# One-layer hybrid trunk on one core: the gated branch's token weights loaded through the ring of raw weights, and half of the Toeplitz copies issued from GpSimd's queue

## The chip, the cores and the metric

The kernel runs on one core of one Trainium2 chip. The metric is the device time of one execution in microseconds, given as the median of several runs. The engines are named as the profile names them: PE is TensorE (matrix multiplies), DVE is VectorE, ACT is ScalarE, POOL is GpSimd, SP is SyncE. PEld is TensorE's weight load, and SPq and ACTq are the instructions on the queues of SP and ACT that issue transfers.

## What is computed

One layer of a sequence model on x of 2048 positions by 1024 channels, in float32. Three branches share one projection; their outputs are normalised, joined and multiplied by W_out, and a mixture of experts follows.

```python
def hybrid_mixer(h, ...):
    z = rms_norm(h, norm_g) @ w_in
    y_a = mixer_spatial_gating(z[..., OFF_A_U:OFF_A_V], z[..., OFF_A_V:OFF_B_X],
                               a_v_norm_g, a_spatial_w, a_spatial_b)
    y_b = mixer_rglru(z[..., OFF_B_X:OFF_B_G], z[..., OFF_B_G:OFF_C_X], ...)
    y_c = mixer_s5(z[..., OFF_C_X:IN_COLS], ...)
    y = jnp.concatenate([rms_norm(y_a, ...), rms_norm(y_b, ...), rms_norm(y_c, ...)], axis=-1)
    return y @ w_out

def mixer_spatial_gating(u_raw, v_raw, v_norm_g, w_s, b_s):
    """per head, within blocks of 128 positions: u * (W_s v + b)"""
    ...
    w = jnp.where(mask[None], w_s, 0.0)      # chunk-causal mask, chunks of 64
    sv = jnp.einsum("hij,bnjhd->bnihd", w, v) + b_s.T[:, :, None]
    return u * sv.reshape(bsz, seq, A_WIDTH)

h = h + hybrid_mixer(h, ...)
h = h + hierarchical_moe(rms_norm(h, norm_ffn_g), ...)   # 16 experts, two of them for each position
```

`w_s` is `a_spatial_w`, six matrices of 128 x 128 (384 KB in all): the token weights of the gated branch A. Branch B is a short convolution and a gated linear recurrence, branch C a complex diagonal state-space layer (S5), which the kernel computes in pieces of 8 positions: inside a piece with a small block Toeplitz matrix, between pieces with a scan.

## The kernel before

**Stages.** x comes in as sixteen tiles of 128 positions and is normalised and transposed (tiles `xT`). Then come the projections by w_in in seven column chunks for each half of 1024 positions, the first half in the order A0, C0, B0, B1, B2, A1, A2. A projection is a group of 24 matmuls in lines 90 to 92 (`split3`: a float32 product as three reduced ones, over eight pieces of the depth); their outputs are called `z`, with shapes 128x512 for B and C and 128x276 for A1. The W_out phase with the router follows, and from about 770 us on the experts.

**What sets the order.** Every engine runs its instructions in the order in which the program wrote them, and waits where an operand isn't ready. The order is written by a main loop over the chunks, which between groups of matmuls gives turns ("ticks") to generators that write the other work piece by piece. A table `TURNS`, keyed by a generator's number and its step, holds back some steps by so many ticks. The generators that matter here:

- `wgen` (generator 1) loads each chunk's raw weights in two halves of 512 KB from SP's queue (`load_w_raw`, L189 to L196) into a pool `raw` with two buffers, and splits them into a high part by ACT (L212) and a low part by DVE (L171, a helper that also serves other lines). For some chunks GpSimd adds 20 router columns (L219 and a subtraction).
- `s5_consts` (L391) computes the constants of branch C and writes them to DRAM tables: `cstP` and `cstT`, and `kpad`, the padded kernel of the Toeplitz matrix. Eight transfers at L738 then spread `kpad` into slot 2 of `cstP`, each 16 x 16 x 128 floats from DRAM to DRAM; those with an odd number go from ACT's queue, the even ones from SP's. After them it loads `a_spatial_w` by two transfers on SP (L742) into two work tiles `big`, gives up eight ticks, transposes the six matrices on PE (L747), copies them to `wsT` on DVE (L748) and zeroes the masked quarter on DVE (L749). It then sets "s5c".
- `c_batch` (L778) works through branch C in eight batches. Each one reads its tables back on SP: `cpp` (L782), `ct` (L783) and, one tick later, `cpm` (L786, slots 2 to 4 of `cstP`, so it needs all eight Toeplitz transfers). On PE stand then the transposes of `zk` (L790, evicted by ACT at L791 to `cx`), the products with `cpp` (L796, "u"), on DVE the scan, on PE the outputs with `cpm` (L815 to L817, "y", evicted by ACT at L818 to `yt`) and a small swap (L825).
- `b_post` (L899) evicts branch B's `z` (ACT L914, `bgg`), multiplies by two gate matrices (PE L920, `bd`), evicts these by ACT (L921, `btr` and `bti`), scans on DVE, and sums squares on PE with a column of ones (L945), for which ACT first squares (L941).
- `c_post` (L831) ends a half of branch C: transposes of `yt` (L851), their eviction (L852, `yc`), the GLU matmuls (L860), sums (L877).

The main loop waits for "s5c" before it begins chunk A1 of the first half.

**DRAM tables and order of transfers.** A transfer that reads a table waits, at its issue, for the landing of those that wrote it. An engine that waits at an issue holds all that stands behind it in its own order, be it transfers or arithmetic.

The code that issues the copies and loads the token weights:

```python
for s in range(8):
    (A if s % 2 else nc.sync).dma_start(out=cstP[s * 16:(s + 1) * 16, 2, :, :], ...)
done.add("s5t")
for h in range(2):
    ws = big[h].rearrange("p (h j) -> p h j", j=P)[:, 0:3, :]
    nc.sync.dma_start(out=ws, in_=io["a_spatial_w"][0, h * 3:h * 3 + 3].rearrange("h i j -> i h j"))
yield 8
```

Of the kernel before, what the change touches and what calls it, by code (L numbers as in the profile page):

```python
# [9 lines left out]
F32 = mybir.dt.float32  # L10
# [3 lines left out]
AF = mybir.ActivationFunctionType  # L14
# [5 lines left out]
P = 128  # L20
# [71 lines left out]
    nc.tensor.matmul(ps, al, bh, start=False, stop=last)  # L92


TURNS = {(32, 2): 0, (40, 12): 0, (1, 119): 5, (29, 3): 5, (21, 4): 3, (13, 4): 1, (17, 14): 3, (28, 6): 2, (26, 7): 3, (17, 2): 0, (33, 1): 2, (12, 9): 3, (25, 7): 1, (28, 9): 2, (28, 11): 3, (21, 9): 0, (44, 4): 0, (35, 97): 3, (32, 3): 0, (48, 9): 1, (38, 4): 0, (41, 2): 2, (14, 6): 1, (18, 15): 2, (37, 1): 3, (1, 132): 0, (48, 5): 0, (35, 85): 2, (9, 1): 0, (44, 8): 0, (49, 7): 2, (27, 8): 2, (29, 1): 2, (25, 3): 0, (47, 11): 5}
RING = 9
NST = 2

# [1 line left out]
class Flow:  # L100
# [12 lines left out]
    def tick(self):  # L113
# [7 lines left out]
        while act:  # L121
            for it in list(act):
                try:
                    r = next(it[0])
                    it[3] += 1
                    r = TURNS.get((it[2], it[3]), r)
                    if r == 0:
# [17 lines left out]
def phases12(tc, io, hd, hc, tab, gcol, ident, c8, stg):  # L145


    nc = tc.nc
    V, A, G, T = nc.vector, nc.scalar, nc.gpsimd, nc.tensor
    ctx = ExitStack()  # L150
    with ctx:
# [7 lines left out]
        rawp = pool("raw", 2)  # L159
        uvp = pool("uvp")  # L160
        psz = pool("psz", 4, space=PSUM)
        pst = pool("pst", 2, space=PSUM)
# [3 lines left out]
        bank = lambda p, nm: p.tile([P, 512], F32, name=nm, tag="b")  # L166
# [22 lines left out]
        def load_w_raw(n):  # L189
            src, cols, _ = chunks[n]  # L190
            m = 256 // len(cols)
            r = []
            for kk in range(2):
                raw = rawp.tile([P, 4, 256], F32, name="raw")
                for j, c in enumerate(cols):
                    nc.sync.dma_start(out=raw[:, :, j * m:(j + 1) * m],  # L196
                                      in_=src[kk * 512:(kk + 1) * 512, c:c + m].rearrange("(k p) n -> p k n", p=P))
                r.append(raw)
            return r

        def wgen():
            for n in range(len(chunks)):
                raws = load_w_raw(n)
                yield
                while begun[0] < n - 1:
                    yield
                w = wp.tile([P, 2, 8, 276], F32R, name="w")
                for k in range(0, 8, 2):
                    rw_ = raws[k // 4][:, k % 4:k % 4 + 2, :]
                    for j in range(2):  # L210
                        g = col(chunks[n][2], k + j)
                        A.activation(w[:, 0, k + j, 0:256], rw_[:, j], AF.Copy, scale=g)  # L212
                    for j in range(2):
                        stt(w[:, 1, k + j, 0:256], rw_[:, j], col(chunks[n][2], k + j), w[:, 0, k + j, 0:256].bitcast(F32), OP.mult, OP.subtract)
                    yield
                if n in routed:
                    while "rw" not in done:
                        yield
                    G.tensor_copy(w[:, 0, :, 256:276], routed[n])  # L219
                    tt(w[:, 1, :, 256:276], routed[n], w[:, 0, :, 256:276].bitcast(F32), OP.subtract, G)  # L220
                wt[n] = w
                if 6 <= n < 14:
                    yield from route_w(n - 6)
            done.add("w")

        def route_w(k):

            raw = rawp.tile([P, 8, P], F32, name="raw")
            nc.sync.dma_start(out=raw, in_=wo[k * P:(k + 1) * P, :].rearrange("p (m n) -> p m n", n=P))
            yield  # L230
            pp_ = []
            for kk in range(2):
                ps = bank(pst if kk else psm, "tp").rearrange("p (k n) -> p k n", n=P)
                for j in range(4):
                    T.transpose(ps[:, j, :], raw[:, kk * 4 + j, :], ident)
                pp_.append(ps)
            for kk in range(2):
                A.activation(raw[:, kk * 4:kk * 4 + 4, :], pp_[kk], AF.Copy)
            yield
            ps = bank(psm, "m")  # L240
            for j in range(8):
                T.matmul(ps[:, 0:20], raw[:, j, :], rw[:, j, :], start=j == 0, stop=j == 7)
            g = col("mix_out_norm_g", k)
            ts(rwy[:, k, :], ps[:, 0:20], g, None, OP.mult)
# [127 lines left out]
        wsT = base.tile([P, 6, P], F32, name="wsT")  # L372
# [14 lines left out]
        cstP = drp.tile([P, 5, 16, P], F32, name="cstP")  # L387
        cstT = drp.tile([P, 2, 16, 129], F32, name="cstT")
        kpad = drp.tile([16, 16, 15, 16], F32, name="kpad")

        def s5_consts(pp):  # L391
# [51 lines left out]
            ps = bank(pst, "tp")  # L443
# [8 lines left out]
            ps = bank(pst, "tp")  # L452
# [154 lines left out]
            for j in range(2):  # L607
                ps = bank(pst, "tp")
# [7 lines left out]
            e = eo[:, 16:19]  # L616
# [76 lines left out]
            big = [big2[:, i * 512:(i + 1) * 512] for i in range(4)]  # L693
# [3 lines left out]
            for g in range(0, 16, 4):  # L697
                dst = lambda slot: cstP[:, slot, g:g + 4, :]

                i = g // 4 % 2  # L700
# [15 lines left out]
                ps = bank(pst, "tp").rearrange("p (a b) -> p a b", b=P)  # L716
# [13 lines left out]
                ps = bank(psm, "tp").rearrange("p (a b) -> p a b", b=P)  # L730
# [4 lines left out]
                nc.sync.dma_start(out=kpad[:, g:g + 4], in_=kp)  # L735
                yield
            for s in range(8):
                (A if s % 2 else nc.sync).dma_start(out=cstP[s * 16:(s + 1) * 16, 2, :, :], in_=kpad[:, :, s:s + 8, :].rearrange("c g t e -> c g (t e)"))  # L738
            done.add("s5t")
            for h in range(2):  # L740
                ws = big[h].rearrange("p (h j) -> p h j", j=P)[:, 0:3, :]
                nc.sync.dma_start(out=ws, in_=io["a_spatial_w"][0, h * 3:h * 3 + 3].rearrange("h i j -> i h j"))  # L742
            yield 8
            for h in range(2):
                ps = bank(pst, "tp").rearrange("p (h j) -> p h j", j=P)
                for j in range(3):
                    T.transpose(ps[:, j, :], big[h][:, j * P:(j + 1) * P], ident)  # L747
                V.tensor_copy(wsT[:, h * 3:h * 3 + 3, :], ps[:, 0:3, :])  # L748
            V.memset(wsT[64:128, :, 0:64], 0.0)  # L749
            done.add("s5c")  # L750
            yield

# [623 lines left out]
        open_pool("prep")  # L1376
        F.add(xprep(2))
        F.add(s5_consts(pools["prep"]))

        def pipeline(lst):  # L1380
# [8 lines left out]
        n = 0  # L1389
# [46 lines left out]
        for h in range(2):  # L1436
            F.until(lambda: ("r", h) in done)
            for m in range(4):
# [4 lines left out]
                for t in range(8):  # L1443
# [16 lines left out]
                    g = h * 8 + t  # L1460
# [499 lines left out]
def trunk(tc, io, out):  # L1960
    nc = tc.nc
    with tc.tile_pool(name="outer", bufs=1) as po, tc.tile_pool(name="c8", bufs=2) as c8, tc.tile_pool(name="odr", bufs=1, space=DRAM) as pd:
        tab = po.tile([P, 368], F32, name="tab")
        gcol = po.tile([P, 8], F32, name="gcol")
        ident = po.tile([P, P], F32, name="ident")
        make_identity(nc, ident)
        hd = pd.tile([S + P, D], F32, name="hd")
        hc = pd.tile([S, D + 16], F32, name="hc")
        stg = []
        phases12(tc, io, hd, hc, tab, gcol, ident, c8, stg)  # L1970
        moe(tc, io, hd, hc, out, tab, gcol, ident, stg)
# [25 lines left out]
```

## Time and profile before

| | |
|---|---|
| time, median of 3 runs | 1603.42 us (1600.23 to 1604.23) |
| the profiled execution | 1600.41 us, of which its span is 1598.6 us |
| PE busy | 1492.4 us, 93% of the span |
| DVE busy | 986.4 us, 62% |
| ACT busy | 864.5 us, 54% |
| POOL busy | 471.1 us, 29% |
| chain that ended last, by engine | PE 74%, DVE 13%, DMA 5%, ACT 4% |

The span is the time from the first to the last recorded instruction; the 1.8 us beside it belong to the same execution. The chain that ended last is followed back from the last instruction to what released each step, so its shares say what the time was spent on, where the busy shares say only how much each engine worked. A row of a timeline gives the start and the length in us, the engine, the line, the operation with output and inputs, and in brackets for how long the engine sat idle before it and which instruction ended that.

### The profile page before, as it was taken

The numbers are of one execution on the slowest core, as the hardware profiler recorded it, in microseconds if no ns is written. First come the engines' busy times: TensorE is split into PE (matmuls) and PEld (weight loads), VectorE is DVE, ScalarE is ACT, GpSimd is POOL, SyncE is SP. The second block draws the span as 40 slices with busy tenths as digits, with TensorE's granted clock in tenths as the row PEclk, the third lists the DMA queues.
The fourth block names the chain that finished last, engine by engine and source line by source line (L and its number), as shares of the span: only waits on it lengthen the run. The fifth ranks groups of instructions, "written<-read, shape, count | busy, mean of one in ns | idle before, by whom it ended". The sixth has DMA issues, their size and how long they took to land.

```text
span 1598.6 us, 25576 instructions
## 1 busy us (share of the span) xinstructions
PE 1492.4 (93%) x8373; PEld 1286.7 (80%) x8374; DVE 986.4 (62%) x2011; ACT 864.5 (54%) x1913; POOL 471.1 (29%) x396
## 2 busy tenths in 40 slices
PE   7998879999999999997799899999999999999993
PEld 6866678878899989997588678888888888888882
DVE  6588661674543487887879886668888857303001
ACT  6377543677544534312346546666566665666662
POOL 0132000000000000010355436555555555445442
PEclk9999888999999999998799899999999999999997
DMA  6247632313532726707577887679888877534342
GB/s 179 66 92 139 188 113 76 123 53 105 166 106 73 264 80 233 281 28 265 200 226 233 248 254 202 201 209 278 269 234 230 250 218 209 139 71 111 89 111 77
DMA packets 213774, 267.46 MB, mean 167 GB/s; under 512 B 34824, under 2 KB 178384, under 8 KB 213648
## 3 DMA queue, kind: packets, MB, share of 16 engines
q1 hardware_dynamic: 187808, 201.95, 39.9%
q0 software_dynamic: 24480, 62.27, 16.1%
q10 hardware_dynamic: 1360, 1.57, 0.3%
q8 instruction: 78, 1.28, 0.3%
q14 instruction: 48, 0.39, 0.1%
HBM read 217.09 MB, written 76.94 MB: 184 GB/s over the span
## 4 chain that ended last, share of the span: by engine, by line
PE 74%; DVE 13%; DMA 5%; ACT 4%; issue 2%; SPq 1%; POOL 0%; POOLq 0%; ACTq 0%; DVEq 0%
PE pg L1688 23%; PE z L90 8%; PE z L92 8%; PE z L91 8%; PE pd L1729 4%; PE pd L1728 4%; PE pd L1727 4%; DMA stg<-in_expert_w_up_dram 2%; DVE ring L1614 2%; DVE ring L1596 2%; PE pt L1695 2%; DVE w L171 1%; PE m L920 1%; PE pt L1700 1%; PE ph L1695 1%
## 5 line engine op out<-in xcount | busy, mean ns | idle before, releaser
L1688 PE MATMUL pg<-ring,xs 128*128 x2016 | 487.3, 394 | 11.8 <-DVE ring L1614 10.6
L1688 PEld LDWEIGHTS pg<-ring,xs 128*128 128x128 f32 x2016 | 378.1, 189 | 91.6 <-issue 14.0
L90 PE MATMUL z<-w,xT 128*128 128x256 f32 (+1 forms) x848 | 250.2, 295 | 4.5 <-DVE ht L171 3.2
L92 PE MATMUL z<-w,xT 128*128 128x256 f32 (+1 forms) x848 | 244.3, 288 | 7.2 <-DVE xT L169 7.2
L91 PE MATMUL z<-w,xT 128*128 128x256 f32 (+1 forms) x848 | 244.3, 288 | 0.0
L1596 DVE TENSOR_SCALAR ring<-stg,gcol 128x512 fp32r<-128x512 f32 x242 | 128.5, 592 | 164.8 <-PE pg L1688 86.2
L1614 DVE SCALAR_TENSOR_TENSOR ring<-stg,gcol,ring 128x512 fp32r<-128x512 f32 x248 | 222.2, 956 | 0.0
L92 PEld LDWEIGHTS z<-w,xT 128*128 128x128 f32 x848 | 163.8, 193 | 8.5 <-DVE xT L169 8.5
L90 PEld LDWEIGHTS z<-w,xT 128*128 128x128 f32 x848 | 164.2, 194 | 7.7 <-issue 4.2
L91 PEld LDWEIGHTS z<-w,xT 128*128 128x128 f32 x848 | 164.4, 194 | 1.4 <-issue 1.4
L1727 PE MATMUL pd<-ring,hh 128*128 x336 | 132.1, 393 | 1.7 <-DVE hh L1633 1.7
L1728 PE MATMUL pd<-ring,hh 128*128 x336 | 131.7, 392 | 0.0
L1729 PE MATMUL pd<-ring,hh 128*128 x336 | 131.7, 392 | 0.0
L1892 POOL DMA_INDIRECT hd<-yb,tab x41 | 76.9, 1874 | 182.5 <-ACT yb L1831 182.5
L171 DVE SCALAR_TENSOR_TENSOR w<-raw,vec,w 128x256 fp32r<-128x256 f32 x176 | 82.0, 511 | 61.9 <-ACT w L212 61.8
L1941 POOL TENSOR_TENSOR yb<-yb,gf 128x1024 f32<-128x1024 f32 x40 | 116.9, 2923 | 2.5 <-ACT hu L1856 2.5
L1906 POOL TENSOR_TENSOR hs<-hs,hu 128x256 f32<-128x256 f32 x84 | 99.8, 1188 | 54.4 <-ACT hu L1810 53.7
L90 PE MATMUL z<-xT,w 128*128 128x512 f32 x256 | 110.5, 432 | 0.2 <-ACT xT L298 0.2
L212 ACT ACTIVATE w<-raw,vec 128x256 fp32r<-128x256 f32 x176 | 77.2, 497 | 59.9 <-PE z L92 36.5
L171 DVE SCALAR_TENSOR_TENSOR ht<-z,rsd,ht 128x256 f32<-128x256 f32 x176 | 85.1, 484 | 29.2 <-PE z L92 21.3
L91 PE MATMUL z<-xT,w 128*128 128x512 f32 x256 | 102.2, 399 | 0.2 <-DVE xT L169 0.2
L92 PE MATMUL z<-xT,w 128*128 128x512 f32 x256 | 102.0, 398 | 0.0
(440 smaller groups left out, 2576.7 us busy)
## 6 DMA issues: line engine op xcount, KB each, us to landing
stg<-in_expert_w_gate_dram SPq DMA_DIRECT2D x62, 512.0 KB, 4.3
stg<-in_expert_w_up_dram SPq DMA_DIRECT2D x62, 512.0 KB, 5.8
stg<-in_expert_w_down_dram SPq DMA_DIRECT2D x60, 512.0 KB, 4.5
raw<-in_w_in_dram SPq DMA_DIRECT2D x48, 256.0 KB
raw<-in_w_out_dram SPq DMA_DIRECT2D x24, 512.0 KB
ht<-in_x_dram SPq DMA_DIRECT2D x16, 512.0 KB
yp<-yTd SPq DMA_DIRECT2D x8, 1024.0 KB
hd<-ht SPq DMA_DIRECT2D x16, 512.0 KB
```

What stands on the lines that cost most here:

```text
L90: nc.tensor.matmul(ps, ah, bh, start=first, stop=False)
L91: nc.tensor.matmul(ps, ah, bl, start=False, stop=False)
L92: nc.tensor.matmul(ps, al, bh, start=False, stop=last)
L171: stt = lambda o, a, s, b, o0, o1: V.scalar_tensor_tensor(out=o, in0=a, scalar=s, in1=b, op0=o0, op1=o1)
L1596: x = v.tensor_scalar(out=ring[:, r, 0, sl], in0=src[:, sl], scalar1=g, scalar2=None, op0=OP.mult)
L1614: x = v.scalar_tensor_tensor(out=ring[:, r, 1, sl], in0=src[:, sl], scalar=g, in1=hi, op0=OP.mult, op1=OP.subtract)
L1688: i = t.matmul(pg[f], xx[j // 2], w[j % 2], start=k == 0 and j == 0, stop=k == 7 and j == 2)
L1727: t.matmul(pd[n], hh[:, 0, kf], w[0], start=kf == 0, stop=False)
L1728: t.matmul(pd[n], hh[:, 0, kf], w[1], start=False, stop=False)
L1729: i = t.matmul(pd[n], hh[:, 1, kf], w[0], start=False, stop=kf == 3)
L1906: g.tensor_tensor(out=o, in0=o, in1=hu[:, f * 256:(f + 1) * 256], op=OP.mult).then_inc(s_hm, 1)
L1941: g.tensor_tensor(out=z, in0=z, in1=gf, op=OP.mult).then_inc(p_z, 1)
```

## The change

The token weights are loaded earlier and elsewhere. `wgen` gets a step `spatial_w` after its chunk 2 (B0): it takes a buffer of the pool `raw`, loads all six matrices with one transfer on SP, and a turn later transposes them on PE and evicts them with two ACT copies to `wsT`; DVE zeroes the quarter there. The two loads, the eight ticks, the six transposes, the two DVE copies and the zeroing leave `s5_consts`. The four Toeplitz copies that ACT issued are issued by GpSimd. Two keys of `TURNS` are renumbered by one, since generator 1 has one step more.

```diff
-TURNS = {..., (1, 119): 5, ..., (1, 132): 0, ...}
+TURNS = {..., (1, 120): 5, ..., (1, 133): 0, ...}
...
                 wt[n] = w
                 if 6 <= n < 14:
                     yield from route_w(n - 6)
+                if n == 2:
+                    yield from spatial_w()
             done.add("w")
+
+        def spatial_w():
+
+            raw = rawp.tile([P, 8, P], F32, name="raw")
+            nc.sync.dma_start(out=raw[:, 0:6, :], in_=io["a_spatial_w"][0].rearrange("h i j -> i h j"))
+            yield
+            for h in range(2):
+                ps = bank(pst, "tp").rearrange("p (h j) -> p h j", j=P)
+                for j in range(3):
+                    T.transpose(ps[:, j, :], raw[:, h * 3 + j, :], ident)
+                A.activation(wsT[:, h * 3:h * 3 + 3, :], ps[:, 0:3, :], AF.Copy)
+            V.memset(wsT[64:128, :, 0:64], 0.0)
...
             for s in range(8):
-                (A if s % 2 else nc.sync).dma_start(out=cstP[s * 16:(s + 1) * 16, 2, :, :], ...)
+                (G if s % 2 else nc.sync).dma_start(out=cstP[s * 16:(s + 1) * 16, 2, :, :], ...)
             done.add("s5t")
-            for h in range(2):
-                ws = big[h].rearrange("p (h j) -> p h j", j=P)[:, 0:3, :]
-                nc.sync.dma_start(out=ws, in_=io["a_spatial_w"][0, h * 3:h * 3 + 3].rearrange("h i j -> i h j"))
-            yield 8
-            for h in range(2):
-                ps = bank(pst, "tp").rearrange("p (h j) -> p h j", j=P)
-                for j in range(3):
-                    T.transpose(ps[:, j, :], big[h][:, j * P:(j + 1) * P], ident)
-                V.tensor_copy(wsT[:, h * 3:h * 3 + 3, :], ps[:, 0:3, :])
-            V.memset(wsT[64:128, :, 0:64], 0.0)
             done.add("s5c")
             yield
```

The changed kernel's lines are numbered 14 higher from the new function to the end of `s5_consts` (L738 becomes L752) and 4 higher behind it. The order on ACT where the last constants of branch C are written, before (`bxc`, `btr` and `bti` are tiles of branch B):

```order
L914 ACTIVATE bgg<-z 128x512
L212 ACTIVATE w<-raw,vec 128x256 x2
L738 DMA cstP<-kpad 16x16x128 x4
L941 ACTIVATE bxc<-bgg 128x512
L921 ACTIVATE btr<-m,b_cols 128x512
L921 ACTIVATE bti<-m,b_cols 128x512
```

Now ACT's four issues are gone from between the weights' split and the squaring, and the same four stand on GpSimd behind the zeroing of `kp`, ahead of the router columns of chunk A1's weights (`w<-rw`) and the state updates of branch C (`gst`):

```order
L169 TENSOR_TENSOR m_1501<-m_1501,m_1500 128x576
L743 MEMSET kp 16x4x112
L752 DMA cstP<-kpad 16x16x128 x4
L219 CAST w<-rw 128x8x20
L169 TENSOR_TENSOR w<-rw,w 128x8x20
L169 TENSOR_TENSOR gst<-gst,gtmp 128x2 x8
```

The order on PE at the beginning of chunk A1, before:

```order
L796 MATMUL m<-cx,cpp 128x128 x4
L790 MATMUL tp<-ident,zk 128x128 x2
L747 MATMUL tp<-ident,big_337 128x128 x6
L815 MATMUL m<-cpm,cx 128x128
...
L825 MATMUL tp<-cg,swp 128x2
L796 MATMUL m<-cx,cpp 128x128 x4
L790 MATMUL tp<-ident,zk 128x128 x2
L920 MATMUL m<-bxc,bd 128x512 x2
L90 MATMUL z<-w,xT 128x276
```

and after it:

```order
L800 MATMUL m<-cx,cpp 128x128 x4
L794 MATMUL tp<-ident,zk 128x128 x2
L90 MATMUL z<-w,xT 128x276
...
L819 MATMUL m<-cpm,cx 128x128
...
L829 MATMUL tp<-cg,swp 128x2
L800 MATMUL m<-cx,cpp 128x128 x4
L794 MATMUL tp<-ident,zk 128x128 x2
L924 MATMUL m<-bxc,bd 128x512 x2
L90 MATMUL z<-w,xT 128x276
```

The transposes of the token weights have left, and A1's first group of 24 matmuls stands in their place; behind `bd` stands its second group. At A1's end the order before has a group between the transposes of `yt` and the GLU matmuls:

```order
L851 MATMUL tp<-ident,yt 128x128 x8
L90 MATMUL z<-w,xT 128x276
...
L92 MATMUL z<-w,xT 128x276
L860 MATMUL m<-yc,glu 128x512 x8
```

and after it has none there:

```order
L92 MATMUL z<-w,xT 128x276
L855 MATMUL tp<-ident,yt 128x128 x8
L864 MATMUL m<-yc,glu 128x512 x8
L881 MATMUL m<-ones,yc 128x1 x16
```

A1's last group has moved ahead of the transposes of `yt`. The six transposes now stand on PE inside chunk B0, twelve matmuls behind those of L610:

```order
L92 MATMUL z<-xT,w 128x512
L236 MATMUL tp<-ident,raw 128x128 x6
L90 MATMUL z<-xT,w 128x512
```

On SP the load of `a_spatial_w` stands between the raw weights of chunk 2 and those of chunk 3, and the two loads at L742 are gone from between the Toeplitz copies and the first tables of branch C.

## Rows read from the trace of the kernel before

**Rows 1.** The page's view of the span in 40 equal slices (40 us each): PE's busy share and its granted clock, in tenths.

```profile
PE   7998879999999999997799899999999999999993
PEclk9999888999999999998799899999999999999997
```

**Rows 2.** The view of windows. Columns: the window in us, its length, busy time (and instructions) of PE, PEld, DVE, ACT and POOL, PE's granted clock as a share of full speed, the busy share of the transfer engines, GB/s.

```profile
60.00:80.00 20.00, 20.00 (x90) 16.21 (x89) 12.14 (x62) 4.18 (x9) 6.51 (x17) 1.00 0.18 54
155.00:160.00 5.00, 3.80 (x15) 2.45 (x13) 0.00 (x0) 0.00 (x0) 0.00 (x0) 1.00 0.90 172
160.00:165.00 5.00, 0.63 (x3) 0.64 (x4) 0.00 (x0) 1.89 (x4) 0.00 (x0) 0.68 1.09 175
165.00:170.00 5.00, 5.00 (x15) 4.21 (x16) 1.64 (x4) 4.94 (x7) 0.00 (x0) 0.50 0.79 212
170.00:175.00 5.00, 5.00 (x20) 3.96 (x19) 3.74 (x10) 2.81 (x7) 0.00 (x0) 0.80 1.04 323
...
280.00:720.00 440.00, 432.19 (x3078) 396.82 (x3078) 280.30 (x724) 218.67 (x502) 8.63 (x25) 0.99 0.41 137
```

**Rows 3.** The timeline of ACT from 150 us on, around its Toeplitz issues (ACTq).

```profile
153.02 0.90 ACT L212 ACTIVATE w<-raw,vec 128x256 fp32r<-128x256 f32 x2
157.90 5.16 ACTq L738 DMA_DIRECT2D cstP<-kpad  x4
163.11 0.63 ACT L941 ACTIVATE bxc<-bgg 128x512 f32<-128x512 f32 x1 [9.19 <-DMA cstT<-ang]
...
164.21 0.68 ACT L921 ACTIVATE bti<-m,b_cols 128x512 f32<-128x512 f32 x1
```

**Rows 4.** The timeline of PE in the same stretch: the gate matmuls, the sums of squares, and the u products of the first two batches of branch C.

```profile
154.15 1.88 PE L920 MATMUL m<-bxc,bd 128*128 128x512 f32 x4
...
164.37 1.87 PE L945 MATMUL m<-ones,bxc 128*128 128x1 f32 x8 [5.57 <-ACT btr L921]
...
177.41 1.05 PE L796 MATMUL m<-cx,cpp 128*128 128x128 f32 x8
...
183.63 1.05 PE L796 MATMUL m<-cx,cpp 128*128 128x128 f32 x8
```

**Rows 5.** The timeline of DVE there: the weights' low part, and the first batch's state products (`cv`).

```profile
165.32 0.88 DVE L171 SCALAR_TENSOR_TENSOR w<-raw,vec,w 128x256 fp32r<-128x256 f32 x2 [10.89 <-ACT w L212]
...
179.03 0.75 DVE L169 TENSOR_TENSOR cv<-m,ct 128x256 f32<-128x256 f32 x2
```

**Rows 6.** The timeline of SP's queue there: its four Toeplitz issues, and the issues of the first batch's tables.

```profile
157.90 7.00 SPq L738 DMA_DIRECT2D cstP<-kpad  x4
...
166.25 0.37 SPq L782 DMA_DIRECT2D cpp<-cstP  x1
...
167.99 0.44 SPq L786 DMA_DIRECT2D cpm<-cstP  x1
```

**Rows 7.** The view of one tile: the gathers of the experts' inputs, transfers that GpSimd issues (duration of the instruction in ns, min/median/max, of 45), and the time from their issue to the landing.

```profile
L1888 POOL DMA_INDIRECT xg<-hc,tab x45: 980/1002/1868, 773.0 to 1556.1; - x45
...
DMA to landing us min/median/max: 4.2/5.9/8.1
```

**Rows 8.** The view of one line: ACT's four Toeplitz issues (ns, min/median/max).

```profile
L738 ACTq DMA_DIRECT2D cstP<-kpad x4: 517/610/862, 157.9 to 162.5; - x4
```

**Rows 9.** The timeline of POOL: the router columns of chunk A1's weights.

```profile
149.97 0.67 POOL L219 CAST w<-rw 128x160 fp32r<-128x160 f32 x1 [6.60 <-PE z L92]
```

**Rows 10.** The timeline of PE where the token weights are transposed, up to A1's first group.

```profile
196.85 0.38 PE L790 MATMUL tp<-ident,zk 128*128 128x128 f32 x2
...
199.59 0.55 PE L747 MATMUL tp<-ident,big 128*128 128x128 f32 x3 [1.34 <-DVE gtmp L169]
...
204.34 0.38 PE L825 MATMUL tp<-cg,swp 128*128 128x2 f32 x2 [2.86 <-DVE wsT L748]
...
207.19 0.69 PE L90 MATMUL z<-w,xT 128*128 128x276 f32 x1
```

**Rows 11.** The timeline of DVE there.

```profile
203.73 1.02 DVE L748 COPY wsT<-tp 128x384 f32<-128x384 f32 x2
...
205.28 0.16 DVE L169 TENSOR_TENSOR gtmp<-tp,cs 128x2 f32<-128x2 f32 x1
```

**Rows 12.** The timelines of ACT and PE behind it: the eviction that begins the next chain, and the PE work that waits for that chain's end.

```profile
213.58 0.38 ACT L791 ACTIVATE cx<-tp 128x256 f32<-128x256 f32 x1 [1.01 <-PE tp L790]
...
230.08 1.87 PE L945 MATMUL m<-ones,bxc 128*128 128x1 f32 x8 [5.35 <-ACT yt L818]
```

**Rows 13.** The timelines of ACT and PE at A1's end: the eviction of `yc`, the first matmul of A1's last group, and the GLU.

```profile
254.53 1.09 ACT L852 ACTIVATE yc<-tp 128x512 f32<-128x512 f32 x2 [2.14 <-PE tp L851]
...
254.69 0.38 PE L90 MATMUL z<-w,xT 128*128 128x276 f32 x1
...
257.83 7.03 PE L860 MATMUL m<-yc,glu 128*128 128x512 f32 x16
```

**Rows 14.** The timelines of PE, SP and ACT near the place to which the transposes move: four transposes between projection matmuls, the issue of raw weights (eight transfers), and chunk 3's split.

```profile
71.42 0.60 PE L610 MATMUL tp<-ident,big 128*128 128x128 f32 x4
71.77 0.48 PE L90 MATMUL z<-xT,w 128*128 128x512 f32 x1
...
41.71 32.51 SPq L196 DMA_DIRECT2D raw<-in_w_in_dram  x8
...
84.44 1.70 ACT L212 ACTIVATE w<-raw,vec 128x256 fp32r<-128x256 f32 x4
```

More of the change, by code (lines that the diff above doesn't have):

```diff
@@ L92, in split3 @@
     nc.tensor.matmul(ps, al, bh, start=False, stop=last)
-TURNS = {(32, 2): 0, (40, 12): 0, (1, 119): 5, (29, 3): 5, (21, 4): 3, (13, 4): 1, (17, 14): 3, (28, 6): 2, (26, 7): 3, (17, 2): 0, (33, 1): 2, (12, 9): 3, (25, 7): 1, (28, 9): 2, (28, 11): 3, (21, 9): 0, (44, 4): 0, (35, 97): 3, (32, 3): 0, (48, 9): 1, (38, 4): 0, (41, 2): 2, (14, 6): 1, (18, 15): 2, (37, 1): 3, (1, 132): 0, (48, 5): 0, (35, 85): 2, (9, 1): 0, (44, 8): 0, (49, 7): 2, (27, 8): 2, (29, 1): 2, (25, 3): 0, (47, 11): 5}
+TURNS = {(32, 2): 0, (40, 12): 0, (1, 120): 5, (29, 3): 5, (21, 4): 3, (13, 4): 1, (17, 14): 3, (28, 6): 2, (26, 7): 3, (17, 2): 0, (33, 1): 2, (12, 9): 3, (25, 7): 1, (28, 9): 2, (28, 11): 3, (21, 9): 0, (44, 4): 0, (35, 97): 3, (32, 3): 0, (48, 9): 1, (38, 4): 0, (41, 2): 2, (14, 6): 1, (18, 15): 2, (37, 1): 3, (1, 133): 0, (48, 5): 0, (35, 85): 2, (9, 1): 0, (44, 8): 0, (49, 7): 2, (27, 8): 2, (29, 1): 2, (25, 3): 0, (47, 11): 5}
 RING = 9
@@ L737, in s5_consts @@
             for s in range(8):
-                (A if s % 2 else nc.sync).dma_start(out=cstP[s * 16:(s + 1) * 16, 2, :, :], in_=kpad[:, :, s:s + 8, :].rearrange("c g t e -> c g (t e)"))
+                (G if s % 2 else nc.sync).dma_start(out=cstP[s * 16:(s + 1) * 16, 2, :, :], in_=kpad[:, :, s:s + 8, :].rearrange("c g t e -> c g (t e)"))
             done.add("s5t")
-            for h in range(2):
-                ws = big[h].rearrange("p (h j) -> p h j", j=P)[:, 0:3, :]
-                nc.sync.dma_start(out=ws, in_=io["a_spatial_w"][0, h * 3:h * 3 + 3].rearrange("h i j -> i h j"))
-            yield 8
-            for h in range(2):
-                ps = bank(pst, "tp").rearrange("p (h j) -> p h j", j=P)
-                for j in range(3):
-                    T.transpose(ps[:, j, :], big[h][:, j * P:(j + 1) * P], ident)
-                V.tensor_copy(wsT[:, h * 3:h * 3 + 3, :], ps[:, 0:3, :])
-            V.memset(wsT[64:128, :, 0:64], 0.0)
             done.add("s5c")
```

## The prediction

> **What bounds the kernel now.** I first read the page's slices [rows 1]: PE is busy nearly everywhere at full clock, so a saving on another engine counts only where PE waits for it. PE's share falls and its clock sags in the fourth and fifth slices (120 to 200 us, which hold the constants of branch C) and in the sixth (200 to 240). I then read those stretches as windows and engine by engine. From 280 to 720 us PE is busy 432.19 of 440 us at a clock of 0.99 [rows 2]: what is gained before 280 us is carried to the end, because behind it PE works through a fixed amount without waiting.
>
> The first hole lies at 158 to 164 us. ACT ends its last weight split at 153.92 (153.02 + 0.90), then has nothing to compute until 163.11: the four Toeplitz issues, which begin at 157.90 and take 5.16 us, stand in its order [rows 3]. They are ahead of the eviction `btr`, and PE stands 5.57 us waiting for just that [rows 4]; DVE stands 10.89 us for ACT's next split [rows 5]. Afterwards PE's granted clock is 0.68, 0.50 and 0.80 in three windows of 5 us, where it had been full before [rows 2]: PE fell to the lower of its two levels, 1.2 GHz, after having idled. The second hole lies around 200 us: PE waits 1.34 us ahead of the second half of the token weights' transposes and 2.86 us for DVE's work behind them [rows 10].
>
> **The Toeplitz issues leave ACT.** The squaring at 163.11 can start when the split ends, and `btr` and `bti` when their gate matmuls are done: these start at 154.15 and last 1.88, so end at 156.03 [rows 4]. `bti` then starts at about 156.1 in place of 164.21: 8.1 us earlier [rows 3]. DVE's chain (`w`, recurrence, `cv` at 179.03 [rows 5]) hangs on ACT's and moves as much, `cv` to 170.9. PE alone could gain more: the 5.57 us, and in the windows at 0.50 and 0.80 half of 5 and a fifth of 5 us, together 9.1. But it meets DVE's and ACT's chain again in the batches, so I take the smaller, **8.1 us**.
>
> What is late next there? The tables of branch C. The first batch's `cpp` is issued at 166.25, behind SP's own Toeplitz issues, which start at 157.90 and take 7.00 [rows 6]. Their transfers don't start earlier than now, since all wait for `kpad`. With two fewer loads behind them, `cpp` is issued some 1 us or more sooner, and the first u, now at 177.41 [rows 4], has to wait for it only from 169.3 on. That leaves about 4 us from an issue at 165 for the landing; the gathers take 4.2 at the least from issue to landing [rows 7], so nothing to a microsecond is lost here.
>
> **The same issues on GpSimd.** No row shows such a transfer from GpSimd; the nearest are the gathers, 1.00 us each by the median and 1.87 at most, landing 4.2 to 8.1 us after issue [rows 7]. Four from 157.90 end between 161.9 and 165.4, and the last lands between 165 and 173. Behind them on GpSimd stands the router columns' cast, now at 149.97 [rows 9], which moves to about 162 to 166 and is read first by A1's matmuls, now at 207.19 and after the change near 197: 30 us of cover. The wait that counts is SP's: `cpm` of the first batch waits for all eight landings, and behind it on SP stand the second batch's `cpp` and `ct` and the next raw weights. `cpm` is now issued at 167.99 [rows 6]; the second u, which needs the `cpp` behind it, is at 183.63 [rows 4] and moves to 175.5. With 2.5 to 3 us from the last landing to a landed `cpp`, by the row's ends it is between 7 us early and 1 us late. I put this at **0**, with a transfer of 1.0 us as the median row has it; for a transfer of D us and the longest landing the wait is 4D − 6.5. Each holds 256 pieces of 512 bytes against a gather of 128 rows, which is why D may be above the rows: a rival below.
>
> **The transposes leave the place at 197 us.** In the order A1's first 24 matmuls take their place. They cost 257.83 − 254.69 = 3.14 us [rows 13], and run while PE waits 1.34 and 2.86 us now [rows 10]. DVE is rid of the two copies and the zeroing, 205.28 − 203.73 = 1.55 us [rows 11], ahead of the state's `gtmp` for which PE's next batch waits. Walked through from 196.85: A1's first group to 200.1, the outputs, the swap (which waits for the scan of the batch), the next u and `zk` to 203, the second gate matmul to 205.4 (it waits for DVE's `cv`), A1's second group to 208.5, the outputs and the next u to 211.2. The eviction `cx`, now at 213.58, comes at 211.4. From there an unchanged chain on ACT and DVE leads to the sums at 230.08, where PE waits 5.35 us for its end [rows 12]. So that wait stays, and all behind it is **2.2 us** earlier, with one group of A1 more already done. Bounds: 0, if the chain's other branch (the weights' split, which doesn't move with `cx`) ends last; 4.2, if all of both waits went.
>
> **A1's end.** Since one group is ahead, the GLU no longer stands behind the last group (at 257.83) but directly behind the transposes of `yt`, and waits for their eviction, which ends at 254.53 + 1.09 = 255.62 [rows 13]: **2.2 us** more, between 0 and 3.1 (the group itself).
>
> **The load through the ring.** The buffer that the spatial load takes is set free about 65 us and its transfer is done before 75; SP issues the raw loads around it from 41.71 to 74.2 [rows 14], and DRAM traffic is low there (share 0.18 [rows 2]). Chunk 3's second half has to wait for the buffer until the transposes have read it, about 76, and is read at 84.44 [rows 14]: covered by some 8 us less the transfer. The six transposes stand in a stretch where PE has no gap (20.00 of 20.00 us [rows 2]). Four like them take 0.35 us from their start to the next matmul's, which itself takes 0.48 instead of 0.39 us [rows 14]: 0.43 for four, so **0.65 us lost** for six, carried to the end. The two ACT copies lie beside an ACT busy 4.18 of 20 us there [rows 2], the zeroing on DVE beside 12.14 of 20; both are far ahead of their reader. That's nothing, or 1.5 us at most if the chain of chunk 3's weights ended last. The `TURNS` keys only keep their places.
>
> **The sum.** 8.1 + 2.2 + 2.2 − 0.65 = 11.9 us. From the profiled execution's own 1600.41 that gives 1588.5. This execution lies 3.0 below the median of 1603.42; the prediction is for a median, so 1603.4 − 11.9 = **1591.5**.
>
> **Rivals.** (1) *GpSimd's copies are late by a little.* If each takes 1.7 to 2.8 us (about the gather's longest, to 1.5 times it), the second u waits 4D − 6.5, 0.3 to 4.7 us, and PE falls to the lower clock again, some 2.5 us as in the window at 0.50 [rows 2]. Gain 9 to 4.8, time 1594.4 to 1598.6, say **1597**. For it: twice the pieces of a gather. Against: a gather also has to read its row numbers, and the median is 1.00. The Trainium skill, "SBUF — State Buffer", section "A bandwidth-pool intuition that's wrong (but worth ruling out)", adds that a transfer from GpSimd is starved while VectorE copies (0.62 us alone, 3.1 overlapped); no row here shows that pair, and by 3.1 the sum would be 11.9 − 5.9 − 2.5 = 3.5 us, an estimate by that page.
>
> (2) *Only issuing time is saved.* If the wait in the hole is that of the tables' round trip, the batches can't start sooner, whichever queue issues: ACT is rid of 4 × 0.61 = 2.4 us [rows 8], less the 0.65 of the transposes, and the later groups only fill the waits that remain: gain 1.8, time **1601.6**. For it: the releaser named at ACT's 9.19 us is a transfer of the tables, and the transfer engines are at 1.09 and 0.79 [rows 2]. Against: ACT's and DVE's work that stands behind the issues is branch B's and the weights', which reads no table. The Trainium skill, "DMA: Bandwidth & Descriptors", section "Issuing engines are not separate DMA queues", says just this: starting transfers from several engines saves only the issuer's time, usually small. ACT's row of 9.19 us idle speaks against it here, since an issuer that computes also loses what it waits for.
>
> (3) *Slower: GpSimd's copies hold SP.* One mechanism: the copies, written one after the other on GpSimd, take D each; SP stands at `cpm` until the last has landed, with all tables and raw weights behind it, and PE stands at the second u for 4D − 6.5 plus 2.5 of clock. The gain is gone from D = 4.0 on (16 − 6.5 + 2.5 = 12.0), and the time is over 0.3% longer from D = 5.2. At D = 6 it is 17.5 + 2.5 − 11.9 = 8.1 slower, **1611.5**. For it: nobody has shown what such a copy costs there. Against: it needs over 2.7 times the longest gather [rows 7].
>
> **How the numbers follow.** The forecast, gain 9 to 15 us (1588.4 to 1594.4): 0.60. Rival 1: 0.20. Rival 2, and copies of 2.8 to 5.2 us with it, which end within 4.8 us of now: 0.11. Rival 3: 0.06. More than 15, if PE keeps its full 9.1 and both waits at 200 go: 0.03. A measurement of this kernel can tell about 0.3%, 4.8 us, from no change. So faster 0.60 + 0.20 + 0.03 = 0.83, same 0.11, slower 0.06. The range reaches from 1586, for the bigger gain, to 1598, which takes in most of rival 1, and leaves some 0.19 out.
>
> **What would show it.** Right: no ACTq issue at 154 to 163; `bti` at about 156; no PE wait of 5.57 there and a clock near 1.00 in 160 to 175; four POOL issues of 1 to 2 us each from about 158; `cpm` issued before 172; `wsT` evicted by ACT near 75; PE's sums still waiting 5 us at about 218; a wait of 1 us ahead of the GLU. Wrong: PE waiting for `cpp` at the first or second u (rival 1 or 3 by the length of GpSimd's issues; rival 2 if those are short and tables land late), or PE waiting for chunk 3's weights near 85 to 95 us, which would say that the ring's buffer was held too long.

## The result, and the profile after

The changed kernel takes 1590.12 us (median of 7 runs, 1587.26 to 1594.48) where the kernel before took 1602.13 (7 runs, 1600.23 to 1605.28) on the same chip: a ratio of 0.9926 with a 95% interval of 0.9908 to 0.9944, 12.0 us faster. The profiled execution takes 1590.12 us, its span 1588.3: 10.3 less than the profiled execution before.

The page's slices, PE and its granted clock, beside [rows 1]:

```profile
PE   7998989999999999996899899999999999999993
PEclk9999988999999999998899999999999999999996
```

The windows (columns as in [rows 2]):

```profile
70.00:80.00 10.00, 8.84 (x44) 6.98 (x44) 7.38 (x34) 2.18 (x5) 4.00 (x7) 1.00 0.32 93
...
155.00:160.00 5.00, 5.00 (x20) 3.42 (x19) 2.15 (x5) 4.04 (x7) 0.00 (x0) 1.00 0.91 228
160.00:165.00 5.00, 5.00 (x27) 4.22 (x26) 1.64 (x4) 4.95 (x7) 2.87 (x6) 1.00 0.89 144
165.00:170.00 5.00, 5.00 (x24) 4.09 (x23) 3.48 (x9) 4.01 (x9) 0.53 (x1) 1.00 0.96 221
170.00:175.00 5.00, 3.58 (x19) 2.45 (x18) 4.90 (x10) 2.09 (x5) 0.00 (x0) 1.00 0.95 269
```

The hole at 158 to 164 us is gone, and with it the low clock behind it: 1.00 in all three windows from 160 on, against 0.68, 0.50 and 0.80. But the first line is new: PE, which had no gap from 60 to 80 us [rows 2], is busy for 8.84 of 10 us. ACT's timeline, to be read against [rows 3], and PE's, against [rows 4]:

```profile
156.39 0.90 ACT L212 ACTIVATE w<-raw,vec 128x256 fp32r<-128x256 f32 x2
157.19 0.62 ACT L945 ACTIVATE bxc<-bgg 128x512 f32<-128x512 f32 x1
...
159.44 0.69 ACT L925 ACTIVATE bti<-m,b_cols 128x512 f32<-128x512 f32 x1 [0.17 <-PE m L924]
```

```profile
157.53 1.88 PE L924 MATMUL m<-bxc,bd 128*128 128x512 f32 x4
162.02 0.95 PE L949 MATMUL m<-ones,bxc 128*128 128x1 f32 x8
...
171.44 1.05 PE L800 MATMUL m<-cx,cpp 128*128 128x128 f32 x8
...
175.18 1.10 PE L924 MATMUL m<-bxc,bd 128*128 128x512 f32 x2 [1.61 <-DVE cv L169]
178.88 1.05 PE L800 MATMUL m<-cx,cpp 128*128 128x128 f32 x8
```

The gate matmuls begin 3.38 us later than before, at 157.53, but the second u products 4.75 us earlier, at 178.88. Between them lie 21.35 us where there were 29.48: the removal of ACT's issues is worth 8.13. The late beginning comes from three places: 0.50 is there before any edit acts (the transposes at 71.42 stand at 71.92), 2.06 arise at the six moved transposes, and 0.8 at a lower clock around 145 us. The rows of the second one, from PE and DVE:

```profile
71.92 0.60 PE L624 MATMUL tp<-ident,big 128*128 128x128 f32 x4
...
76.45 0.88 PE L236 MATMUL tp<-ident,raw 128*128 128x128 f32 x6 [1.16 <-DVE big L170]
```

```profile
75.57 0.43 DVE L169 TENSOR_TENSOR big<-big 128x256 f32<-128x256 f32 x1 [1.79 <-POOL big L169]
75.91 0.48 DVE L170 TENSOR_SCALAR big<-tp,sgn 128x256 f32<-128x256 f32 x1
76.31 0.41 DVE L170 TENSOR_SCALAR big<-tp 128x256 f32<-128x256 f32 x1
```

The transposes at 71.92 wrote two banks `tp` (the buffers that take PE's transposes); DVE is to read both, but stands in its own order behind a step that waits 1.79 us for GpSimd. The six transposes want the same two banks, so PE stands 1.16 us until DVE has emptied them. The windows of the third, each from the gate matmuls near 140 us to the next sums, first before, then after (granted clock 0.69 and 0.59):

```profile
137.97:143.29 5.32, 5.32 (x15) 3.60 (x16) 5.28 (x8) 4.38 (x6) 3.75 (x3) 0.69 0.99 139
```

```profile
140.55:146.66 6.11, 6.11 (x14) 4.17 (x15) 6.07 (x12) 5.17 (x7) 3.81 (x3) 0.59 1.01 124
```

GpSimd's issues (timeline, and the view of the line with the time to landing), and SP's, against [rows 6]:

```profile
162.04 2.54 POOL L752 DMA_DIRECT2D cstP<-kpad  x4 [16.11 <-DMA kpad<-kp]
164.58 0.33 POOL L219 CAST w<-rw 128x160 fp32r<-128x160 f32 x1
```

```profile
L752 POOL DMA_DIRECT2D cstP<-kpad x4: 562/586/832, 162.0 to 164.0; - x4
...
DMA to landing us min/median/max: 5.7/5.9/6.3
```

```profile
161.75 2.54 SPq L752 DMA_DIRECT2D cstP<-kpad  x4
168.03 0.36 SPq L786 DMA_DIRECT2D cpp<-cstP  x1
...
170.05 0.37 SPq L790 DMA_DIRECT2D cpm<-cstP  x1
```

An issue costs GpSimd 0.59 us, and the 16.11 us for which it stands there hold nobody: the cast behind it is read some 27 us later. Further on, PE's sums and the GLU, against [rows 12] and [rows 13]:

```profile
223.23 1.87 PE L949 MATMUL m<-ones,bxc 128*128 128x1 f32 x8 [5.29 <-ACT yt L822]
...
247.44 1.03 PE L855 MATMUL tp<-ident,yt 128*128 128x128 f32 x8
248.31 7.03 PE L864 MATMUL m<-yc,glu 128*128 128x512 f32 x16
```

The sums are 6.85 us earlier than before, 2.10 more than at the second u; the GLU 9.52, another 2.67. At the span's end it is 10.3.

### The profile page after: what moved, and what is told of

The parts are those of the page before. It is cut to its first block, busy times and chain, and to the rows that moved or that the text cites. A ratio compares the mean times of both kernels' runs of the same rounds, so it can differ in the third digit from the quotient of the medians.

```text
span 1588.3 us, 25588 instructions
## 1 busy us (share of the span) xinstructions
PE 1489.4 (94%) x8373; PEld 1283.5 (81%) x8374; DVE 976.4 (61%) x2009; ACT 865.6 (54%) x1915; POOL 484.6 (31%) x400
## 4 chain that ended last, share of the span: by engine, by line
PE 74%; DVE 13%; DMA 4%; ACT 4%; issue 2%; POOL 1%; SPq 0%; DVEq 0%; POOLq 0%; ACTq 0%
PE pg L1692 24%; PE z L90 8%; PE z L92 8%; PE z L91 8%; PE pd L1733 4%; PE pd L1732 4%; PE pd L1731 4%; DMA stg<-in_expert_w_up_dram 3%; DVE ring L1600 2%; PE pt L1699 2%; DVE ring L1618 2%; DVE ht L171 1%; DVE w L171 1%; PE m L924 1%; DVE xT L169 1%
## 5 line engine op out<-in xcount | busy, mean ns | idle before, releaser
L1618 DVE SCALAR_TENSOR_TENSOR ring<-stg,gcol,ring 128x512 fp32r<-128x512 f32 x248 | 213.9, 923 | 0.0
L1910 POOL TENSOR_TENSOR hs<-hs,hu 128x256 f32<-128x256 f32 x84 | 106.5, 1268 | 50.1 <-ACT hu L1814 47.8
```

The lines of the kernel that those rows point to most:

```text
L1618: x = v.scalar_tensor_tensor(out=ring[:, r, 1, sl], in0=src[:, sl], scalar=g, in1=hi, op0=OP.mult, op1=OP.subtract)
L1910: g.tensor_tensor(out=o, in0=o, in1=hu[:, f * 256:(f + 1) * 256], op=OP.mult).then_inc(s_hm, 1)
```

## Experiments

Each was timed beside the kernel before, which took 1600.90 us beside the four from "changed again" to "other banks", 1599.46 beside the next three and 1601.22 beside the last two; so the times are compared by their ratios. As the time of a run scatters by several us, three distances on PE, between starts, carry the reading: from the transposes at 71 us to the next (L624 to L732; L610 to L718 in the numbering before), from the gate matmuls at 157 to the second u, and from there to the GLU, with the sums on the way. In us:

| kernel | time, median | ratio to before (95%) | 71 us to next transposes | gate matmuls to second u | second u to sums | second u to GLU |
|---|---|---|---|---|---|---|
| before | | | 23.45 | 29.48 | 46.45 | 74.20 |
| changed | 1590.12 | 0.9926 (0.9908 to 0.9944) | 25.51 | 21.35 | 44.35 | 69.43 |
| changed again | 1590.29 | 0.9933 (0.9913 to 0.9953) | 25.48 | 21.35 | 44.36 | 69.43 |
| queue only | 1592.95 | 0.9949 (0.9931 to 0.9967) | 23.45 | 21.85 | 49.43 | 76.35 |
| ring only | 1597.61 | 0.9972 (0.9953 to 0.9992) | 25.48 | 28.57 | 44.36 | 69.06 |
| other banks | 1585.48 | 0.9908 (0.9888 to 0.9927) | 24.10 | 21.34 | 44.36 | 68.10 |
| sixteen issues | 1590.24 | 0.9950 (0.9935 to 0.9965) | 25.48 | 21.62 | 44.36 | 69.16 |
| all on SP | 1591.20 | 0.9950 (0.9933 to 0.9968) | 25.48 | 21.35 | 44.36 | 69.55 |
| group back | 1589.09 | 0.9946 (0.9928 to 0.9963) | 25.51 | 21.37 | 42.14 | 69.59 |
| copies on ACT | 1598.32 | 0.9982 (0.9967 to 0.9997) | 23.45 | 28.07 | 44.04 | 71.97 |
| banks and group | 1587.49 | 0.9917 (0.9896 to 0.9938) | 24.11 | 21.35 | 42.12 | 69.22 |

**The changed kernel again.** No edit.

> The changed kernel once more, as a yardstick for the three beside it: 1590 us (1587 to 1594), 12 below the kernel before. If the late start of 0.5 us at 72 us and the lower clock at 140 to 150 us of its first profile are chance, this profile has them otherwise; if they belong to the change, it has the same.

It gave 1590.29. Its transposes at 71 us start at 71.52, so 0.4 of the late start was chance; over all runs they start between 70.75 and 72.19. The low clock at 145 us came again: 6.06 us from the gate matmuls at 140 to the sums, against 6.11 in the first profile and 5.32 in the kernel before.

**The queue alone**, in the kernel before:

```diff
-                (A if s % 2 else nc.sync).dma_start(out=cstP[s * 16:(s + 1) * 16, 2, :, :], ...)
+                (G if s % 2 else nc.sync).dma_start(out=cstP[s * 16:(s + 1) * 16, 2, :, :], ...)
```

> The kernel before with the four Toeplitz issues on GpSimd, nothing else. Theory (ACT was held by the wait for kpad and by the four issues, and PE and DVE by ACT): 8.1 us gained, 1594, the first u products about 8 to 9 us earlier, A1's first group still behind the transposes at 197 with the waits of 1.3 and 2.9 us. Rival (only issuing time is saved): 4 x 0.6 = 2.4 us, 1599.7. Rival (the batches' tables end last): the first u stays near 177, under 3 us gained.

The time fell by 8.0 us, to 1592.95, and the distance to the second u by 7.63. That excludes the rival of 2.4 us: the interval's weak end is 5.3 us. That 8.0 and 7.63 agree so well is partly chance, since 2.15 us of the gain are lost again before the GLU (76.35 against 74.20), and the profiled execution, 1595.29 us, is 5.1 faster than the one before. Two things came out on the way. The first u now waits for transfers, because nothing shifted it later (timeline of PE):

```profile
170.59 1.13 PE L796 MATMUL m<-cx,cpp 128*128 128x128 f32 x8 [1.95 <-DMA yTd<-bgg]
```

The releaser named is a store; of what stands around it on SP, the u reads `cpp`, so I take it for that table's landing. And PE's second hole, now at 190 to 200 us, takes the clock down to the lower level, where it had stayed at 1.00 before (windows of this run, then of the kernel before at its hole):

```profile
190.00:195.00 5.00, 3.19 (x19) 2.70 (x18) 4.83 (x14) 1.66 (x4) 0.20 (x1) 0.83 0.58 184
195.00:200.00 5.00, 2.95 (x14) 2.89 (x14) 3.48 (x11) 0.38 (x1) 0.20 (x1) 0.50 0.45 133
200.00:205.00 5.00, 5.00 (x18) 2.93 (x17) 2.88 (x9) 2.56 (x5) 0.00 (x0) 0.65 0.33 102
```

```profile
195.00:200.00 5.00, 2.83 (x23) 2.27 (x22) 4.86 (x13) 2.04 (x5) 0.20 (x1) 1.00 0.38 115
200.00:205.00 5.00, 2.14 (x20) 1.95 (x19) 4.79 (x13) 0.38 (x1) 0.00 (x0) 1.00 0.42 123
```

The lower clock makes its distance to the sums 3 us longer than before.

**The ring alone**: the changed kernel, its four issues on ACT again.

```diff
-                (G if s % 2 else nc.sync).dma_start(out=cstP[s * 16:(s + 1) * 16, 2, :, :], ...)
+                (A if s % 2 else nc.sync).dma_start(out=cstP[s * 16:(s + 1) * 16, 2, :, :], ...)
```

> The changed kernel with the four Toeplitz issues back on ACT: the move of the token weights alone. Theory (A1 one group earlier is worth 2.2 + 2.7 us, the transposes at 76 us cost 2.1 us, and up to 0.8 more by the clock): a net gain of 2 to 3 us, 1599 to 1600, with the wait of about 9 us on ACT back. Rival (the loss at 76 us is hidden in the wait for the tables): 4.9 us gained, 1597. Rival (the two parts need each other): no gain, 1602.

The time is 1597.61, 3.3 below its kernel before, between the first two expectations and unable to choose. The profile does: ACT's hole is back (28.57), the transposes at 76 us cost the same 2.03, and behind the second u the full 5.1 us are gained. The row of ACT, to be read against [rows 3]:

```profile
163.62 0.63 ACT L945 ACTIVATE bxc<-bgg 128x512 f32<-128x512 f32 x1 [8.29 <-DMA cstT<-ang]
```

The parts don't need each other: 8.0 and 3.3 make 11.3, and the whole change gave 10.6 beside them.

**Other banks**: the six transposes write to the second pool of PSUM.

```diff
-                ps = bank(pst, "tp").rearrange("p (h j) -> p h j", j=P)
+                ps = bank(psm, "tp").rearrange("p (h j) -> p h j", j=P)
```

> The changed kernel with the two PSUM banks of the token weights' transposes taken from the other pool, whose order on every engine is the same. Theory (the transposes wait 1.16 us because VectorE hasn't drained the two banks of the first pool, being held by GpSimd's big): that wait is gone, the 0.9 us of work stays, 1.2 us gained on the changed kernel, 1589, and by chance the lower clock at 140 to 150 us too. Rival (the wait is for the load of the weights or for something else that lies before them): the wait stays at 1.2 us, the time at 1590.

The wait is gone (timeline of PE), and the distance from 71 us falls from 25.48 to 24.10:

```profile
74.50 0.82 PE L236 MATMUL tp<-ident,raw 128*128 128x128 f32 x6
```

What is left over the 23.45 of before is 0.65 us for six transposes. So the wait was for the banks and cost 1.4 us. The time is 1585.48, 4.8 below "changed again", and the intervals of the two overlap. Of the difference only these 1.4 are explained. The profiled executions lie further apart, 1582.62 against 1589.76: there 1.3 lie in a shorter stretch from the sums to the GLU where the clock was higher, 2.1 between the GLUs of the two halves, and 3.1 behind the second one. From its start (468 to 483 us) to that of the experts' last products the profiles here last between 1089.2 us (this one) and 1095.8 (the queue alone), 1092.3 in "changed again" and 1095.4 in "banks and group", which has the same banks. So this part isn't shown to be the banks'.

**Sixteen issues**: each of GpSimd's copies cut into four.

```diff
-                (G if s % 2 else nc.sync).dma_start(out=cstP[s * 16:(s + 1) * 16, 2, :, :], in_=kpad[:, :, s:s + 8, :]...)
+                for gs in ([slice(g, g + 4) for g in (0, 4, 8, 12)] if s % 2 else [slice(0, 16)]): (G if s % 2 else nc.sync).dma_start(out=cstP[s * 16:(s + 1) * 16, 2, gs, :], in_=kpad[:, gs, s:s + 8, :]...)
```

> The changed kernel with each of GpSimd's four Toeplitz copies cut into four, sixteen issues for the same bytes. Theory (SP stands at cpm until the last of GpSimd's copies has landed; four issues of 0.6 us leave it 5 us of slack at the second u): at 0.6 us for each the last issue comes 7 us later, cpm is issued at about 177 in place of 170, the second u waits 2 to 3 us for its table, and with the clock behind it the time is 3 to 5 us longer than the changed kernel's, 1593 to 1595, 6 to 9 below the kernel before. Rival (an issue costs by its pieces, so sixteen small ones cost no more than four): cpm stays near 170, no change from 1590. Rival (the clock is lost at every wait there): 1597 or more.

The view of the line, and SP's timeline:

```profile
L752 POOL DMA_DIRECT2D cstP<-kpad x16: 513/516/787, 145.2 to 170.1; - x16
```

```profile
172.05 0.36 SPq L790 DMA_DIRECT2D cpm<-cstP  x1
```

My theory missed. An issue of a quarter costs nearly as much as a whole one (0.52 against 0.59 us), so the rival's reason is wrong too; but three of the first copy's quarters need only earlier parts of `kpad` and went out at 145 us, so the dose was smaller than meant. GpSimd also stood 2.85 us ahead of its last five issues, until one of its own earlier transfers had landed. The last issue, at 170, moved `cpm` by 2.9 us only, counted from the gate matmuls (15.45 us behind them against 12.52). The second u hardly noticed (21.62): there the tables had nearly 3 us to spare. How long four such copies would have to be before SP holds PE isn't settled by this run; at 0.59 us each, with those 3 us in hand, it isn't reached.

**All on SP**: no Toeplitz copy on ACT or GpSimd.

```diff
-                (G if s % 2 else nc.sync).dma_start(out=cstP[s * 16:(s + 1) * 16, 2, :, :], ...)
+                (nc.sync).dma_start(out=cstP[s * 16:(s + 1) * 16, 2, :, :], ...)
```

> The changed kernel with all eight Toeplitz copies on SP, none on GpSimd or ACT. Theory (what counts is that ACT doesn't stand at the issues; which queue issues them then costs only what it delays behind them): ACT's wait is gone as in the changed kernel, the first table is issued 2 to 3 us later than 168, the first u waits for it, 1 to 2.5 us longer than the changed kernel, 1591 to 1593. Rival (GpSimd's own queue makes the transfers themselves sooner): 5 us or more longer, 1595 or later, with the tables landing that much later.

SP takes 7.80 us for the eight, the first table goes out 11.83 us behind the gate matmuls instead of 10.50, and the first u waits for it (timelines of SP and PE):

```profile
161.89 7.80 SPq L752 DMA_DIRECT2D cstP<-kpad  x8
169.80 0.54 SPq L786 DMA_DIRECT2D cpp<-cstP  x1
```

```profile
172.76 1.13 PE L800 MATMUL m<-cx,cpp 128*128 128x128 f32 x8 [0.70 <-DMA cpp<-cstP]
```

At the second u nothing is left of it (21.35), for PE then waits less for DVE's `cv` (0.66 us against 1.61). By its ratio, 0.9950, the time is no different from the changed kernel's. GpSimd's queue shows no merit of its own; what counts is that ACT doesn't stand at the issues.

**The group back**: A1's first group behind the second gate matmul again.

```diff
-            done.add("s5c")
+            yield 8; done.add("s5c")
```

> The changed kernel with eight ticks of generator 'constants' put back before it lets chunk A1 begin, so that A1's first group stands behind the second gate matmul as before and its last one between the transposes of yt and the GLU, with the token weights' transposes still early. Theory (most of the 4.8 us behind 192 us is the group itself: 2.1 at the sums, 2.7 at the GLU): the GLU is 3 to 4 us later than in the changed kernel, 251.5, and the time 1593 to 1594. Rival (the gain is VectorE's 1.55 us of copies and the transposes' 0.9 us that left this place, and the group only fills what would be idle): under 1.5 us later, 1590 to 1591.5.

The theory fell. The time is 1589.09, and PE's rows show why:

```profile
220.26 1.86 PE L949 MATMUL m<-ones,bxc 128*128 128x1 f32 x8 [5.35 <-ACT yt L822]
...
247.71 7.03 PE L864 MATMUL m<-yc,glu 128*128 128x512 f32 x16
```

Counted from the second u, the sums come 4.3 us earlier than before (42.14 against 46.45) rather than 2.1, and the GLU is where it was in the changed kernel (69.59 against 69.43). Where the group stands moves 2.2 us from one side of the sums to the other and is worth nothing in all. The gain lies in the transposes and their evictions leaving.

**Copies on ACT**, in the kernel before: the transposes stay at 197 us, their copies leave DVE.

```diff
-                V.tensor_copy(wsT[:, h * 3:h * 3 + 3, :], ps[:, 0:3, :])
-            V.memset(wsT[64:128, :, 0:64], 0.0)
+                A.activation(wsT[:, h * 3:h * 3 + 3, :], ps[:, 0:3, :], AF.Copy)
+            G.memset(wsT[64:128, :, 0:64], 0.0)
```

> The kernel before with the token weights' two copies on ScalarE and the zeroing on GpSimd, the transposes left at 197 us. It splits the 4.8 us gained behind 192 us, since A1's group turned out to be worth nothing. Theory (VectorE's 1.55 us of copies and zeroing stood ahead of the state update that PE's next batch waits for): the wait of 2.86 us falls to about 1.3, the sums at 230.1 come 1.5 us earlier, the rest of the 4.8 belongs to the transposes' own 0.9 us and their waits for banks. Rival (the transposes hold PE until the bank is free, whoever copies): under 0.5 us at the sums. By the time 1598 to 1600, too little to tell from no change.

More than expected: the sums come 2.4 us earlier (44.04 against 46.45). PE's wait of 2.86 us ahead of the swap is wholly gone:

```profile
198.44 0.55 PE L747 MATMUL tp<-ident,big 128*128 128x128 f32 x3 [1.11 <-ACT wsT L748]
...
200.16 0.28 PE L825 MATMUL tp<-cg,swp 128*128 128x2 f32 x2
```

So it wasn't DVE's 1.55 us of work that PE waited for but a bank: the swap writes to the bank that the first copy empties, and DVE reached it only at 203.73 [rows 11], behind a whole batch's scan; the swap starts at 204.34, while the second copy still runs. The remaining 1.9 of the 4.3 go when the transposes leave too. The hole of ACT, ahead of this edit, is shorter in this run as well:

```profile
162.19 0.63 ACT L941 ACTIVATE bxc<-bgg 128x512 f32<-128x512 f32 x1 [7.79 <-DMA cstT<-ang]
```

**Banks and group**: both edits on the changed kernel.

```diff
-                ps = bank(pst, "tp").rearrange("p (h j) -> p h j", j=P)
+                ps = bank(psm, "tp").rearrange("p (h j) -> p h j", j=P)
...
-            done.add("s5c")
+            yield 8; done.add("s5c")
```

> The changed kernel with the transposes' banks from the other pool, as in the run on other banks, and A1's first group back behind the gate matmuls. Theory (the banks' wait is worth 1.2 us and the group nothing): no wait at 75 us, GLU at about 246.5, time 1586 to 1589. Rival (the other-banks run's 4.8 us below the changed kernel is all its own): 1585. Rival (it was chance, and the wait was covered): 1590.

24.11, 21.35 and 69.22 us, the GLU at 245.37 (245.25 with other banks alone), 1587.49 us: the banks' 1.4 again, and again nothing from the group. The two kernels with other banks have the lowest ratios; by their times alone neither is told from the changed kernel.

## Why the prediction was right, and where it wasn't

**ACT's issues, 8.1 us: right.** 8.13 in the profile after. The three kernels that keep the issues on ACT show 28.07 to 29.48 to the second u and those that don't 21.34 to 21.85, so the term is 6.2 to 8.1 by the pair that one picks. The spread of the three is ACT's own idle time, 7.79, 8.29 and 9.19 us: the forecast was worked out from the longest of them. Of the 9.19, ACT stood 3.98 before its first issue (153.92 to 157.90) and 5.16 at the four, which by themselves take 4 x 0.61 [rows 8]. SP's four took 7.00 us beside them [rows 6] and take 2.54 beside GpSimd's; why SP and ACT were slower together no run here shows. The Trainium skill ("DMA: Bandwidth & Descriptors", section "Issuing engines are not separate DMA queues") says that transfers run on the same engines whoever starts them, and that starting them from several saves only the time of starting. The runs agree with the first half: transfers started by SP alone give the same time as those by SP and GpSimd. The second half prices only the starting, here 2.4 us; ACT lost three times that, since it also stood for `kpad` with arithmetic behind it.

**What is late next: right in kind.** The tables are next in line: 1.95 us for the first u in the run of the queue alone, 0.70 with all copies on SP, 0.54 with other banks, nothing in the changed kernel's first profile and at most 0.3 in its second (14.20 us from the gate matmuls against 13.91). At the second u at most 0.5 of it is left.

**GpSimd's price: right, and below the bound.** 0.59 us by the median where I took 1.0; landing after 5.9. Rival 1 needed 1.7 us or more, rival 3 4.0. Four issues take 2.54 us, as SP's do, while DVE works for a third of the window (1.64 of 5 us) with operations that aren't copies. So no run here shows the case of a transfer starved by DVE's copies, of which the Trainium skill speaks ("SBUF — State Buffer", section "A bandwidth-pool intuition that's wrong (but worth ruling out)").

**Transposes leaving 197 us and A1's end, 2.2 + 2.2: the sizes nearly right, two reasons wrong.** 2.10 and 2.67 measured. The walk to `cx` came out: counted from the second u, the `zk` transposes ahead of it come 2.04 us earlier, with the group of 24 matmuls counted as work in place of the waits. The run with the group put back shows what the group is worth. There the sums come another 2.2 us earlier and the GLU stays, so what the group costs ahead of the sums it gives back at A1's end. The two terms are thus one gain, 4.77 at the GLU, from the transposes and their evictions leaving; both waits went, which I had as the upper bound, 4.2. To take the group itself for the gain, as I did before that run, was wrong.

The first wrong reason in the prediction is that of the 2.86 us, "for DVE's work behind them". The row names `wsT`, and I priced DVE's 1.55 us, where PE waited for a bank that DVE emptied late. It spoiled nothing here, since the claim on that bank left with the transposes. The second is the wait of 1 us for `yc`'s eviction ahead of the GLU. The GLU's row shows no wait, and it starts 0.87 us behind the transposes ahead of it (247.44 to 248.31), so the gain at A1's end came nearer to its bound of 3.1 than I said.

**The transposes at 75 us, −0.65: the term that was mis-sized.** What is left in the run on other banks, with no wait, is the forecast 0.65 us. The whole is 2.06: I took a PE without gaps for a place where only work counts, and didn't ask who had the two banks.

**The sum.** 8.13 + 2.10 + 2.67 − 2.06 − 0.8 of clock − 0.5 of start = 9.5 at the GLU, and 10.3 at the end; forecast 11.9, measured 12.0 by the medians. The last agreement is partly luck: the stretch from the second half's GLU to the end differs by over 6 us between profiles, more than the terms that I missed, 2.7 in all.

**What stays open.** The clock near 145 us. PE waits 4.04 or 4.05 us for DVE ahead of it in every profile, and the stretch behind lasts 5.12 to 6.44 us. "Ring only" and the changed kernel have the same order on every engine up to there, and show 5.35 and 6.11; "banks and group" and "other banks" likewise, 5.12 and 6.44. So neither the ring nor the banks alone decide it, and the 0.8 in the sum may be chance. What does decide it wasn't found.

## What to carry to other kernels

A transfer's issue that waits for an earlier transfer belongs on an engine whose next work is far off: it costs the issuer what stands behind it, not the 0.6 us of issuing. Moving a transpose or matmul moves a claim on a PSUM bank; look up who emptied that bank last, and what stands ahead of that reader in its own order, at the new place as at the old. And where a row says that PE waits for an engine's small operation, ask whether it waits for the operation's length or for its turn.

## What had not been expected of the hardware

A quarter of a copy costs GpSimd 0.52 us to issue and a whole one 0.59: the price here is by the issue and hardly by the bytes. And the same hole can cost the clock or leave it: the one around 200 us left it at 1.00 in the kernel before, whose clock had been low at 165, and took it to 0.50 in the run of the queue alone, whose clock had been full throughout 155 to 175. Whether what lay ahead decided that, or chance as perhaps near 145 us, no run here tested.
